# Time-step projection of a hybrid encoder with the tokens stationary and 32 weight columns moving

## The chip, the core and the metric

The kernel runs on one core of a Trainium2 chip. The metric is the device time of one execution in microseconds (us). TensorE (PE) multiplies a stationary tile, which it loads first, with columns that move through it, and sums into banks of PSUM; VectorE (DVE), ScalarE (ACT) and GpSimd (POOL) work on tiles in SBUF and PSUM; SyncE (SP) issues most of the transfers (DMA).

## What is computed

An encoder of two layers over 512 tokens of width 1024, in float32. Each layer has a feed-forward block, three token mixers in parallel (a Mamba-2 state-space branch, an S5 branch, a retention branch) with gates, and a second feed-forward block. The change touches the first step of the state-space branch, which makes one step size `dt` for each token, direction and head:

```python
h = rmsnorm(x, mix_norm[i])
proj = h @ w_in[i]
z, xbc, dt_raw, u, q, k, v, g, gate_logits = jnp.split(proj, split_pts, axis=-1)
...
dt = jax.nn.softplus(dt_raw.astype(f32).reshape(b, s, 2, SSD_HEADS) + dt_bias.astype(f32))
```

`dt_raw` has 2 x 8 = 16 columns out of 6800 of `proj`. From `dt` come the decays of the scan over chunks of 128 tokens.

## The kernel before

The activations lie with the model width on the partitions: `hh[k]` and `hl[k]`, k = 0 to 7, are the high and the low part of 128 rows of the normed input by 512 tokens, in fp32r. Products are made of such parts to keep the precision: `mm3` (L154 to L158) makes high x high, high x low and low x high. Nearly all large projections take a 128 x 128 piece of the weights as the stationary tile and move 512 tokens through it; their rows carry L156, L157 and L158. Weights are loaded by `wload` in pieces of 512 KB, three buffers deep, and split by ACT (`whi`, L149) and DVE (`wlo`, L150).

`ssd` (L507) is the state-space branch. Its weights for `dt`, `wdt`, hold for each k 32 columns, 16 of the high and 16 of the low part. Before the change the 32 columns are the stationary tile, all 512 tokens move, and the result stands with the columns on 32 partitions (`pdt`). ACT copies it to SBUF (`dts`, L525), PE transposes it in four pieces into a second small bank (`ptd`, L528), so that the tokens lie on the partitions, and DVE copies it out (`dt2`, L530). Then DVE adds the halves, scales by the norm (`rtd`) and adds the bias (L532, L534), and works out the softplus with some 40 small operations (L477 to L505), `da` (L540) and its parts. PE sums the decays (L549). Behind it follow six convolutions (`proj_dt`, `pad` L570, L575, transposes L587), the chunk states (L605), and per chunk the stages with `gm` (L626), `e` (L661), the sums of decays (L657) and the product with `e` (L664).

Between these, `hook()` puts one block of the S5 branch at a time (`s5_block`, L992): `mat` comes by DMA, PE forms L1009, DVE and POOL scan, DVE writes `h` (L1036, L1037), PE forms L1041 and L1043. `gates` (L1048) gives projections that fill the time between.

The order of the instructions on each engine is fixed when the program is built: a scheduler lists them by its own estimate of durations. So a change of one step can move others. PSUM has four banks for large products (`mm`), two small ones (`sm`) and one each of `pa` and `pb`.

The column sums of the norm (`norm_fin`, L194) are named in the prediction because of their shape: 128 x 128 of the squares stationary, two columns of ones moving.

Of the kernel before, what the change touches and what calls it, by code (L numbers as in the profile page):

```python
# [10 lines left out]
F32 = mybir.dt.float32  # L11
F32R = mybir.dt.float32r
I32 = mybir.dt.int32
AF = mybir.ActivationFunctionType
# [4 lines left out]
P = 128  # L19
D = 1024  # L20
KD = D // P
S = 512
# [79 lines left out]
class Core:  # L102
# [404 lines left out]
    def ssd(self, i, L, xs, hook=lambda: None):  # L507
        nc = self.nc
# [3 lines left out]
        with self.tc.tile_pool(name="ssd", bufs=1) as sp:  # L512
# [4 lines left out]
            nc.sync.dma_start(wst, w[:, DT0:DT0 + 16].rearrange("(k p) n -> p k n", p=P))  # L517
            wdt = sp.tile([P, KD, 32], F32R, name="dtw2")
            self.split(wdt[:, :, 0:16], wdt[:, :, 16:32], wst)
            pdt = self.bank("sm")  # L520
            for k in range(KD):
                nc.tensor.matmul(pdt[:32], wdt[:, k], self.hh[k], start=k == 0, stop=False)
                nc.tensor.matmul(pdt[:16], wdt[:, k, 0:16], self.hl[k], start=False, stop=k == KD - 1)
            dts = sp.tile([32, S], F32, tag="y", name="dts", bufs=3)
            nc.scalar.activation(dts, pdt[:32], AF.Copy)  # L525
            ptd = self.bank("sm")
            for t in range(NT):
                nc.tensor.transpose(ptd[:, 32 * t:32 * t + 32], dts[:, t * P:(t + 1) * P], self.id[:32, :32])  # L528
            dt2 = sp.tile([P, NT, 2, 16], F32, name="dt2")
            nc.vector.tensor_copy(dt2.rearrange("p t j d -> p (t j d)"), ptd[:, :P])  # L530
            raw = sp.tile([P, NT, 16], F32, name="dtraw")
# [65 lines left out]
            for d, order in ((0, (0, 1, 2, 3)), (1, (3, 2, 1, 0))):  # L597
                for ci in range(3):
                    t, tn = order[ci], order[ci + 1]
# [618 lines left out]
```

## Time and profile before

| | before |
|---|---|
| median of 3 runs | 2577.45 us (2576.88 to 2578.72) |
| profiled execution | 2580.19 us, of which its span 2578.4 us |
| PE busy | 2538.3 us (98%), 12044 matmul records |
| weight loads of PE (PEld) | 2104.0 us (82%) |
| DVE busy | 1514.7 us (59%) |
| ACT busy | 878.3 us (34%) |
| POOL busy | 646.9 us (25%) |
| DMA | 286.34 MB, mean 111 GB/s |

Shares are of the span. PEld runs beside PE. Matmuls follow each other before the one ahead has ended, so a record of 0.39 us can stand for a step of 0.23 us: the distance between starts is what counts. A matmul with plain fp32 operands leaves two records. PEclk is the clock of PE that was granted, as a share of full speed (2.4 GHz); 0.50 is 1.2 GHz.

### The profile page before, as it was taken

How to read it: one execution, taken by the hardware profiler on the slowest of the kernel's cores; microseconds unless marked ns; L12 is line 12 of the kernel's file. 1: busy time of each engine (PE TensorE's matmuls, PEld its weight loads, DVE VectorE, ACT ScalarE, POOL GpSimd, SP SyncE). 2: the span in 40 equal slices, each digit the busy share in tenths (PEclk: the TensorE clock that was granted, in tenths of full speed). 3: DMA queues.
4: the chain of work that ended last, by engine and by line, in shares of the span. 5: the costliest groups of instructions: out<-in, count | busy, mean ns of one | idle time of the engine just before them, and what ended most of it. 6: DMA issues, size and time to landing. Idle time of an engine off the chain costs nothing. (4 is left out here: it accounts for less than half of the span.)

```text
span 2578.4 us, 31738 instructions
## 1 busy us (share of the span) xinstructions
PE 2538.3 (98%) x12044; PEld 2104.0 (82%) x12044; DVE 1514.7 (59%) x2462; ACT 878.3 (34%) x1298; POOL 646.9 (25%) x636
## 2 busy tenths in 40 slices
PE   8999999999999999999999999999999999999998
PEld 6878887778888888888887888887878888888886
DVE  7746746897555644333486377478965556433433
ACT  4324433334333432222333243333343333322222
POOL 3203411462233221011112043105613323210110
PEclk9999999989999999999999999999899999999999
DMA  5434435342423433332334344454324234324322
GB/s 155 128 116 137 145 120 162 115 129 65 130 78 83 119 98 89 106 98 88 102 89 142 113 148 138 132 144 127 108 69 126 82 82 121 100 82 114 98 83 81
DMA packets 451832, 286.34 MB, mean 111 GB/s; under 512 B 29152, under 2 KB 435296, under 8 KB 451680
## 3 DMA queue, kind: packets, MB, share of 16 engines
q1 hardware_dynamic: 447456, 281.26, 36.7%
q10 hardware_dynamic: 4224, 3.06, 0.4%
q8 instruction: 95, 1.56, 0.2%
q14 instruction: 57, 0.47, 0.1%
HBM read 251.24 MB, written 29.88 MB: 109 GB/s over the span
## 5 line engine op out<-in xcount | busy, mean ns | idle before, releaser
L149 ACT ACTIVATE whi<-wst 128x1024 fp32r<-128x1024 f32 (+4 forms) x488 | 451.6, 927 | 1136.0 <-PE ps_mm L157 906.2
L156 PE MATMUL ps_mm<-hh,whi 128*128 128x512 f32 x1936 | 760.6, 393 | 6.4 <-ACT whi L149 3.7
L158 PE MATMUL ps_mm<-hh,wlo 128*128 128x512 f32 x1936 | 763.9, 395 | 2.6 <-DVE wlo L150 2.6
L157 PE MATMUL ps_mm<-hl,whi 128*128 128x512 f32 x1936 | 761.7, 394 | 0.0
L150 DVE TENSOR_TENSOR wlo<-wst,whi 128x1024 fp32r<-128x1024 f32 (+4 forms) x488 | 558.4, 1145 | 247.3 <-ACT whi L149 246.3
L156 PEld LDWEIGHTS ps_mm<-hh,whi 128*128 128x128 f32 x1936 | 366.2, 189 | 84.2 <-ACT whi L149 4.9
L158 PEld LDWEIGHTS ps_mm<-hh,wlo 128*128 128x128 f32 x1936 | 365.8, 189 | 79.4 <-DVE wlo L150 3.7
L157 PEld LDWEIGHTS ps_mm<-hl,whi 128*128 128x128 f32 x1936 | 365.9, 189 | 77.6 <-issue 1.7
L227 POOL TENSOR_TENSOR sr<-gt,rbc 128x512 f32<-128x512 f32 x88 | 149.1, 1696 | 817.9 <-ACT gt L225 817.9
L158 PE MATMUL ps_mm<-ah,wlo 128*128 128x512 f32 x704 | 275.6, 391 | 3.1 <-DVE wlo L150 3.1
L157 PE MATMUL ps_mm<-al,whi 128*128 128x512 f32 x704 | 274.6, 390 | 0.0
L156 PE MATMUL ps_mm<-ah,whi 128*128 128x512 f32 x704 | 274.1, 390 | 0.0
L229 DVE TENSOR_TENSOR a<-ps_mm,sr 128x512 f32<-128x512 f32 x88 | 60.4, 687 | 178.8 <-PE ps_mm L158 167.5
L158 PEld LDWEIGHTS ps_mm<-ah,wlo 128*128 128x128 f32 x704 | 132.4, 188 | 31.1 <-DVE wlo L150 3.9
L157 PEld LDWEIGHTS ps_mm<-al,whi 128*128 128x128 f32 x704 | 132.4, 188 | 28.2 <-DVE al L162 0.6
L156 PEld LDWEIGHTS ps_mm<-ah,whi 128*128 128x128 f32 x704 | 132.6, 188 | 27.9 <-ACT ah L161 0.7
L224 DVE TENSOR_TENSOR gt<-ps_mm,rbc 128x512 f32<-128x512 f32 x88 | 60.1, 686 | 139.7 <-PE ps_mm L158 139.6
L157 PE MATMUL ps_mm<-wlo,hh 128*128 128x512 f32 x320 | 126.3, 395 | 0.0
L156 PE MATMUL ps_mm<-whi,hh 128*128 128x512 f32 x320 | 125.9, 400 | 0.0
L158 PE MATMUL ps_mm<-whi,hl 128*128 128x512 f32 x320 | 125.5, 392 | 0.0
L245 DVE SCALAR_TENSOR_TENSOR x<-ps_mm,x 128x512 f32<-128x512 f32 x64 | 44.3, 692 | 133.7 <-PE ps_mm L158 133.4
L184 POOL TENSOR_TENSOR sqsum<-sqsum,sqk 128x512 f32<-128x512 f32 x42 | 67.4, 1606 | 191.0 <-ACT sqk L183 190.7
(395 smaller groups left out, 3257.2 us busy)
## 6 DMA issues: line engine op xcount, KB each, us to landing
wst<-in_ffn_w_gate SPq DMA_DIRECT2D x87, 512.0 KB, 3.7
wst<-in_ffn_w_up SPq DMA_DIRECT2D x87, 512.0 KB, 3.7
wst<-in_w_in SPq DMA_DIRECT2D x74, 512.0 KB, 3.7
wst<-in_ffn_w_down SPq DMA_DIRECT2D x64, 384.0 KB, 3.1
wst<-in_ffn_w_down SPq DMA_DIRECT2D x64, 320.0 KB, 3.1
wst<-in_w_in SPq DMA_DIRECT2D x64, 256.0 KB, 3.0
mat<-sd SPq DMA_DIRECT2D x12, 896.0 KB, 5.1
sd<-mat SPq DMA_DIRECT2D x12, 768.0 KB, 5.0
```

The source lines that it names most:

```text
L149: nc.scalar.activation(hi[:, :nk * n], sv, AF.Copy)
L150: nc.vector.tensor_tensor(lo[:, :nk * n], sv, hi[:, :nk * n].bitcast(F32), ALU.subtract)
L156: mm(out, lh, rh, start=first, stop=False)
L157: mm(out, lh, rl, start=False, stop=False)
L158: mm(out, ll, rh, start=False, stop=last)
L184: nc.gpsimd.tensor_tensor(self.sq, self.sq, t, ALU.add)
L224: nc.vector.tensor_tensor(gt, pg, self.rbc, ALU.mult)
L227: nc.gpsimd.tensor_tensor(sr, gt, self.rbc, ALU.mult)
L229: nc.vector.tensor_tensor(a, pu, sr, ALU.mult)
L245: nc.vector.scalar_tensor_tensor(self.x[d], pd, 0.5, self.x[d], ALU.mult, ALU.add)
```

## The change

The 128 tokens of a chunk become the stationary tile, and the 32 columns of `wdt` move. For each of four chunks there are sixteen matmuls, eight with `hh` and 32 columns and eight with `hl` and 16 columns, which sum into 32 columns of one small bank. The result has the tokens on the partitions at once; the bank `pdt`, the copy `dts` and the four transposes are gone. From the copy out of PSUM on all is as before, two lines higher up in the file (L530 becomes L528, L570 becomes L568, and so on).

```diff
-            pdt = self.bank("sm")
-            for k in range(KD):
-                nc.tensor.matmul(pdt[:32], wdt[:, k], self.hh[k], start=k == 0, stop=False)
-                nc.tensor.matmul(pdt[:16], wdt[:, k, 0:16], self.hl[k], start=False, stop=k == KD - 1)
-            dts = sp.tile([32, S], F32, tag="y", name="dts", bufs=3)
-            nc.scalar.activation(dts, pdt[:32], AF.Copy)
             ptd = self.bank("sm")
             for t in range(NT):
-                nc.tensor.transpose(ptd[:, 32 * t:32 * t + 32], dts[:, t * P:(t + 1) * P], self.id[:32, :32])
+                tc_ = slice(t * P, (t + 1) * P)
+                for k in range(KD):
+                    nc.tensor.matmul(ptd[:, 32 * t:32 * t + 32], self.hh[k][:, tc_], wdt[:, k], start=k == 0, stop=False)
+                    nc.tensor.matmul(ptd[:, 32 * t:32 * t + 16], self.hl[k][:, tc_], wdt[:, k, 0:16],
+                                     start=False, stop=k == KD - 1)
```

On PE, in the first layer, before (`dtw` is the tile of `wdt`; the last transposes of the step follow 22 large matmuls later):

```order
L157 MATMUL ps_mm<-hl_3481,whi 128x512
L158 MATMUL ps_mm<-hh_3480,wlo 128x512
L522 MATMUL ps_sm<-hh_3075,dtw_3648 32x512
L523 MATMUL ps_sm<-hl_3076,dtw_3648 16x512
L522 MATMUL ps_sm<-hh_3132,dtw_3648 32x512
L523 MATMUL ps_sm<-hl_3133,dtw_3648 16x512
```

At the same place after:

```order
L157 MATMUL ps_mm<-hl_3481,whi 128x512
L158 MATMUL ps_mm<-hh_3480,wlo 128x512
L524 MATMUL ps_sm<-dtw_3648,hh_3075 128x32
L525 MATMUL ps_sm<-dtw_3648,hl_3076 128x16
L524 MATMUL ps_sm<-dtw_3648,hh_3132 128x32
```

The place is the same; 16 matmuls before and 64 after stand there one behind the other, with nothing between, in both layers.

On DVE, where the result is taken out of PSUM, before (`pad` and `cacc` belong to the first convolution, `spt` to the softplus):

```order
L530 COPY dt_3675<-ps_sm 128x128
L532 TENSOR_TENSOR dtraw<-dt_3675 128x64
L570 TENSOR_TENSOR pad<-ps_mm,rbc 128x512
L534 SCALAR_TENSOR_TENSOR dtraw<-dtraw,rtd,dtb 128x16 x4
L150 TENSOR_TENSOR wlo<-wst,whi 128x1024
L492 TENSOR_SCALAR spt<-dtraw 128x64
L575 SCALAR_TENSOR_TENSOR cacc<-pad,vec_86,cacc 128x512
L493 TENSOR_TENSOR spt<-spt,dtraw 128x64
```

And after, the copy and the piece in which the first `pad` comes:

```order
L528 COPY dt_3716<-ps_sm 128x128
L530 TENSOR_TENSOR dtraw<-dt_3716 128x64
L532 SCALAR_TENSOR_TENSOR dtraw<-dtraw,rtd,dtb 128x16 x4
L492 TENSOR_SCALAR spt<-dtraw 128x64
L493 TENSOR_TENSOR spt<-spt,dtraw 128x64
```

```order
L497 TENSOR_TENSOR spt<-spt 128x64
L498 TENSOR_TENSOR spt<-spt 128x64
L568 TENSOR_TENSOR pad<-ps_mm,rbc 128x512
L500 TENSOR_SCALAR dt<-spt 128x64
L502 SCALAR_TENSOR_TENSOR dt<-dt,spt 128x64
```

The first `pad` has moved from the third place behind the copy to behind 26 operations of the step, and the convolution's operations no longer alternate with the first part of the softplus.

On PE, in the first layer, at the first products with `e`, before (`sst` are chunk states, `rb` the decays):

```order
L657 MATMUL ps_sm<-rb,us_r 128x512 x2
L1043 MATMUL ps_pb<-h,mat_4282 128x64 x2
L1041 MATMUL ps_pb<-uc,mat_4282 128x64
L1043 MATMUL ps_pb<-h,mat_4282 128x64 x2
L1041 MATMUL ps_pb<-uc,mat_4282 128x64
L1043 MATMUL ps_pb<-h,mat_4282 128x64 x2
L1041 MATMUL ps_pb<-uc,mat_4282 128x64
L1043 MATMUL ps_pb<-h,mat_4282 128x64 x2
L1009 MATMUL ps_pa<-uc,mat 128x64 x8
L664 MATMUL ps_sm<-xs,e 128x64 x4
L657 MATMUL ps_sm<-rb,ls_r 128x512 x2
```

After, ahead of the same products:

```order
L157 MATMUL ps_mm<-hl_3365,whi 128x512
L158 MATMUL ps_mm<-hh_3364,wlo 128x512
L156 MATMUL ps_mm<-hh_3422,whi 128x512
L662 MATMUL ps_sm<-xs,e 128x64 x4
L655 MATMUL ps_sm<-rb,ls_r 128x512 x2
L655 MATMUL ps_sm<-rb,us_r 128x512 x2
```

Between the first decays (L655 x4, L657 before) and the products with `e` there now stand 37 large matmuls and one L1039 (L1041 before); the S5 matmuls that stood there have moved to other places.

## Rows read from the trace of the kernel before

**Rows 1.** The page's first table: engine, busy us (share), records.
```profile
PE 2538.3 (98%) x12044; PEld 2104.0 (82%) x12044; DVE 1514.7 (59%) x2462; ACT 878.3 (34%) x1298; POOL 646.9 (25%) x636
```

**Rows 2.** PE's waits from 400 to 650, then 1700 to 1910: total, times, longest.
```profile
PE ps_pb L1043 <- DVE h L1037: 2.2, 3, 1.3
PE ps_sm L664 <- DVE e L661: 1.5, 2, 1.0
PE ps_sm L631 <- DVE gm L626: 1.3, 1, 1.3
...
PE ps_pb L1043 <- DVE h L1037: 2.5, 3, 1.3
PE ps_sm L664 <- DVE e L661: 1.5, 4, 0.7
PE ps_sm L631 <- DVE gm L626: 0.8, 1, 0.8
```

**Rows 3.** Timeline of PE: start, us, line, out<-in, stationary tile, moving tile, count.
```profile
422.15 0.40 PE L522 MATMUL ps_sm<-hh,dtw 128*32 128x512 f32 x1
...
425.85 0.39 PE L156 MATMUL ps_mm<-hh,whi 128*128 128x512 f32 x1
```

**Rows 4.** Timeline of PE at the four transposes.
```profile
430.61 0.39 PE L156 MATMUL ps_mm<-hh,whi 128*128 128x512 f32 x1
430.93 0.43 PE L528 MATMUL ps_sm<-con,dts 32*128 32x32 f32 x4
...
431.86 0.40 PE L156 MATMUL ps_mm<-hh,whi 128*128 128x512 f32 x1
```

**Rows 5.** Timeline of PE at the column sums of the norm (L194).
```profile
413.46 0.25 PE L194 MATMUL ps_sm<-ones_r,sqh 128*128 128x2 f32 x1
...
414.13 0.48 PE L158 MATMUL ps_mm<-hh,wlo 128*128 128x512 f32 x1
```

**Rows 6.** Timeline of PE at fp32r pairs with 64 stationary columns.
```profile
213.07 0.22 PE L156 MATMUL ps_sm<-xh,ch 128*64 128x128 f32 x1
...
213.79 0.44 PE L156 MATMUL ps_mm<-hh,whi 128*128 128x512 f32 x1
```

**Rows 7.** Timeline of PE at small fp32 matmuls, at full and at half clock.
```profile
459.10 1.22 PE L1009 MATMUL ps_pa<-uc,mat 128*128 128x64 f32 x10
460.15 0.39 PE L549 MATMUL ps_sm<-da,ls_r 128*128 128x64 f32 x2
...
1777.48 1.92 PE L1009 MATMUL ps_pa<-uc,mat 128*128 128x64 f32 x8
```

**Rows 8.** Stretches: length, busy us (records) by engine, PEclk, DMA share, GB/s.
```profile
520.00:540.00 20.00, 18.37 (x92) 15.98 (x91) 18.68 (x28) 8.27 (x9) 13.73 (x15) 0.83 0.47 145
560.00:600.00 40.00, 36.00 (x165) 30.68 (x163) 38.37 (x57) 11.43 (x16) 26.45 (x29) 0.83 0.27 79
1770.00:1860.00 90.00, 85.58 (x415) 72.67 (x414) 79.42 (x130) 28.72 (x35) 50.40 (x51) 0.85 0.43 134
```

**Rows 9.** The same view of short stretches.
```profile
526.00:529.00 3.00, 1.82 (x15) 1.68 (x14) 3.00 (x3) 2.97 (x3) 3.00 (x2) 0.94 0.42 111
1776.00:1782.00 6.00, 6.00 (x27) 5.82 (x28) 1.02 (x4) 1.67 (x2) 1.04 (x2) 0.50 0.54 176
423.00:426.00 3.00, 3.00 (x15) 1.45 (x13) 2.00 (x3) 0.18 (x1) 0.00 (x0) 1.00 0.26 97
459.00:462.00 3.00, 3.00 (x30) 2.96 (x28) 2.96 (x4) 2.52 (x3) 0.13 (x2) 1.00 0.05 11
```

**Rows 10.** Timeline of DVE around the copy out of PSUM.
```profile
429.36 1.12 DVE L886 TENSOR_TENSOR uu<-ps_mm,rbc 128x512 f32<-128x512 f32 x1 [2.25 <-DMA ud<-uu]
431.39 0.29 DVE L530 COPY dt<-ps_sm 128x128 f32<-128x128 f32 x1 [0.92 <-PE ps_sm L528]
...
451.29 1.52 DVE L502 SCALAR_TENSOR_TENSOR dt<-dt,spt 128x64 f32<-128x64 f32 x6
```

## Prediction

> **What bounds the kernel now.** I read the engine table of the page first: TensorE (PE) is busy for 2538.3 of 2578.4 us, on 98% of the span, and nothing else comes near [rows 1]. So time added to PE's queue is added to the kernel, unless it falls into one of the few places where PE waits. Next I read the list of PE's waits around the two state-space stages, one in each layer: the three largest on VectorE (DVE) are 2.2 + 1.5 + 1.3 = 5.0 us in the first layer and 2.5 + 1.5 + 0.8 = 4.8 us in the second [rows 2]. They lie behind the changed step, in stretches in which DVE is all but saturated: 18.7 of 20 us, 38.4 of 40 and 79.4 of 90 [rows 8]. In these the granted clock averages 0.83, 0.83 and 0.85, that is 0.17 x 20 + 0.17 x 40 + 0.15 x 90 = 3.4 + 6.8 + 13.5 = 24 us of full-speed PE time not given. The changed step itself runs in a stretch without any PE wait and at clock 1.00 [rows 3, 9]. So the change is judged by what it does to PE's queue there, then by what that does to the clock, and last by what reaches the waits of the state-space stage.
>
> **PE time removed.** Per layer the 16 matmuls of L522 and L523 start at 422.15 and the next large matmul at 425.85: 3.70 us, 0.23 us each [rows 3]. The four transposes stand between large matmuls: from the start at 430.61 to the one at 431.86 three large matmuls take 1.25 us instead of 3 x 0.23 = 0.68, so the transposes cost 0.57 us [rows 4]. Together 4.27 us of PE time per layer go.
>
> **PE time added.** 64 matmuls come, each with a stationary tile of 128 columns of its own and 32 or 16 moving columns. The trace has no such shape, but two neighbours. The column sums of the norm (L194) have the same stationary tile and 2 moving columns: they follow each other at 0.112 us, six steps from 413.46 to 414.13 [rows 5]. The start matrices of the S5 branch and the decay sums (L1009, L549), 64 moving columns and two records for each instruction, run at the same pace: ten records from 459.10 to 460.15, 0.105 us each [rows 7]. Between 2 and 64 moving columns the step doesn't change, so the load of the 128 stationary columns sets it, and 32 columns lie between. The bound from below is a pair with half the stationary columns (64) and 128 moving: twelve of them in 213.07 to 213.79, 0.06 us each [rows 6]. I take 0.114, with a little for the edges: 64 x 0.114 = 7.3 us per layer. Net 7.3 - 4.27 = +3.0 us per layer, **+6.1 us** for both; at 0.06 it would be 3.84 - 4.27 = -0.4 per layer, -0.9 in all.
>
> The Trainium skill speaks for the change here. The page "TensorE: Matmul & The Clock Gate", section "Back-to-back issue gap", gives some 60 cycles, about 25 ns, for a matmul of 1 to 64 moving columns; by that, as an estimate, 64 x 0.025 = 1.6 us, 2.7 us less than now per layer, and the kernel would end near 2572. The 0.112 us of a matmul with 2 moving columns in this trace is against it, since there each matmul brings its own load.
>
> **The clock.** The new run puts 7.3 us of load-paced matmuls with few columns in one piece. In this trace the clock began to fall in 526 to 529 (0.94), where PE was busy for 1.82 of 3.00 us, with 64-column matmuls. More telling is 1776 to 1782: PE is busy without any gap, 6.00 of 6.00 us, nearly all load-paced small matmuls, and the clock stays at 0.50 [rows 9]. So busy time in this form doesn't bring the clock back. Against a fall: 459 to 462, also load-paced and without a gap, kept 1.00 [rows 9]; but that is some 3 us between large matmuls, with twice and four times the moving columns. The new run is twice as long and has fewer columns than any of these, so I expect that the clock falls to 1.2 GHz in it, and comes back after some large matmuls. At 0.50 both sorts slow down: eight L1009 records take 1.92 us [rows 7], twice what they take at 1.00. A fall thus costs half of the low stretch. In windows of 2 us I count five low stretches in the two stages, so the 24 us make 4.8 us each [rows 8]. One in each layer: **+9.6 us**, between 0 (no fall) and 2 x 6.8 = 13.6, by the one that lies in 560 to 600.
>
> **What hides nothing, and what might give back.** The ACT copy (0.59 us) and the second small PSUM bank go; ACT isn't waited for there, I cost that at nothing. On DVE no instruction is added or removed, and the copy out of PSUM (L530), now at 431.39, is freed: the last of the 64 matmuls ends near 429.5 at full clock, near 431 to 433 at half. The third of the `uu` products stands ahead of it on DVE until 430.5 [rows 10], so at best it begins 0.9 us earlier. The order of the changed program puts 26 operations of the softplus chain ahead of the first convolution, where they were interleaved with it one by one. The large matmuls behind the run are later by the 3 us and by the clock's loss, so DVE finds time for this chain before the first `pad`; alone each costs 0.25 us (six in 1.52) [rows 10], some 6 us, about the time that PE needs for the first projection. DVE is then ahead of PE by a few us when the saturated stage begins, and PE's waits on it shrink. Of the 5.0 and 4.8 us I take some 40%, **-4 us**; the bounds are 0 and -9.8.
>
> **The sum.** +6.1 + 9.6 - 4 = +11.7 us. The profiled execution took 2580.2 us, 1.8 outside its span, and is 2.7 above the median of 2577.45 of the three runs; a difference of stages applies to both alike. Forecast 2577.45 + 11.7 = **2589 us**, +0.45%. Its own range: with the cheapest fall (3.4 us in each layer) and all waits gone 6.1 + 6.8 - 9.8 = +3.1, 2580.5; with the dearest and nothing given back 6.1 + 13.6 = +19.7, 2597.
>
> **Rivals.**
> *The clock holds.* PE has no gap in the new run, and 459 to 462 kept 1.00 [rows 9]. Then +6.1 - 4 = +2.1: 2579.6, at most 2583.6. It decides by whether 1.00 stands throughout the run. The same page of the Trainium skill, section "Why this matters for your kernels", asks for no more than that PE isn't left idle between bursts; by that rule this rival is right. The stretch from 1776 to 1782 doesn't agree with it.
>
> *The re-planned stage gives back more than the step costs (faster).* The planner has re-ordered the whole state-space stage; the first four products with `e` (L664), which stood directly behind eight L1009 and ahead of four L657, now have 37 large matmuls between them and the L657 before. If DVE's lead and this fill end all these waits (9.8) and half of the lost clock (12 of 24), 21.8 us come back: 6.1 + 9.6 - 21.8 = -6.1, 2571. It decides where the waits and falls of the stages are cut by more than 15.7 + 5.2 = 21 of their 34 us. Against it: the dense groups of small matmuls are still there, in other places, and DVE has the same work.
>
> *The re-planned stage waits more.* DVE stays saturated, several loads of `mat` have changed places with loads of weights in SyncE's queue, and an order that fits the planner's durations need not fit the chip's: as many waits again as now, +9.8, makes 2577.45 + 15.7 + 9.8 = 2603; with half, 2598.
>
> *The loads hide.* At 0.06 us a matmul and without a fall: -0.9, 2576.6. Only the pairs with half the stationary tile speak for it; L194 speaks against it.
>
> **Chances.** Forecast 0.58, clock holds 0.20, faster by the stage 0.12, more waits 0.08, loads hide 0.02. A measurement of this kernel can tell about 0.2%, 5.2 us, from no change. Slower by more than that: most of the forecast (0.52), more waits (0.08), a quarter of the held clock (0.05): 0.65. Within: 0.06 + 0.15 + 0.02 = 0.23. Faster: 0.12. The range leaves out the faster case and the far end of the waits: 2576 to 2599.
>
> **What would show it.** Right: 64 PE matmuls at 0.11 us in one piece, later at twice that; granted clock below 1.00 within some us of 429 and 1701; the large matmuls behind it at 0.43 us; PE's busy time higher by about 15 us; DVE's copy near 431. Wrong: steps of 0.06 us or less; 1.00 throughout; or PE's waits on `h`, `e`, `gm` and `sst` and the stage's mean clock changed by more than the step itself costs, in which case the order and not the shape has set the result.

## The result

The changed kernel takes 2606.52 us (median of 4 runs, 2602.29 to 2608.74) against 2578.09 of the kernel before beside it (4 runs, 2576.88 to 2579.68): ratio 1.0108, 95% interval 1.009 to 1.0125, slower by 28.4 us. The forecast was 2589 with a range up to 2599. Its direction was right and its size wrong: 28.4 us came where 11.7 were forecast. The traced execution took 2608.74 us with a span of 2606.9.

The engine table of the page after answers rows 1:

```profile
PE 2563.6 (98%) x12132; PEld 2131.7 (82%) x12132; DVE 1517.1 (58%) x2462; ACT 874.4 (34%) x1294; POOL 652.4 (25%) x636
```

PE is busy for 25.3 us more, on 98% of the span as before, and idle for 3.2 us more. In the changed kernel L528 is DVE's copy, L1041 the matmuls with `h`, L662 those with `e`. The timeline of PE in the first layer's run of 64 matmuls, which answers rows 3:

```profile
425.35 0.26 PE L525 MATMUL ps_sm<-dtw,hl 128*128 128x16 f32 x1
425.46 0.35 PE L524 MATMUL ps_sm<-dtw,hh 128*128 128x32 f32 x1
425.64 0.36 PE L525 MATMUL ps_sm<-dtw,hl 128*128 128x16 f32 x1
...
432.05 0.36 PE L525 MATMUL ps_sm<-dtw,hl 128*128 128x16 f32 x1
432.26 0.77 PE L156 MATMUL ps_mm<-hh,whi 128*128 128x512 f32 x1
432.83 0.63 PE L157 MATMUL ps_mm<-hl,whi 128*128 128x512 f32 x1
433.26 0.63 PE L158 MATMUL ps_mm<-hh,wlo 128*128 128x512 f32 x1
```

The steps are 0.11 us until 425.5, then 0.21; the large matmuls behind take 0.43 us from start to start. The windows over the same place (the columns of rows 8; the clock is the third number from the end) show the fall, with PE and its weight loads busy without a gap. They answer rows 9:

```profile
420.00:424.00 4.00, 4.00 (x27) 3.30 (x26) 2.27 (x3) 1.06 (x1) 0.00 (x0) 1.00 0.31 93
424.00:428.00 4.00, 4.00 (x28) 4.00 (x27) 1.75 (x2) 0.00 (x0) 0.00 (x0) 0.69 0.72 223
428.00:432.00 4.00, 4.00 (x20) 4.00 (x21) 1.11 (x1) 0.00 (x0) 0.00 (x0) 0.50 0.30 109
432.00:436.00 4.00, 4.00 (x11) 3.24 (x12) 3.18 (x17) 0.00 (x0) 0.00 (x0) 0.53 0.47 101
436.00:440.00 4.00, 4.00 (x19) 3.27 (x18) 2.81 (x11) 0.56 (x1) 0.00 (x0) 1.00 0.80 96
```

DVE's copy begins at 432.45, somewhat behind the forecast's 431. So far this is the forecast. What the forecast did not have is the state-space stage behind. PE's waits around it, first layer and then second, which answer rows 2:

```profile
PE ps_pb L1041 <- DVE h L1035: 7.4, 5, 2.8
PE ps_sm L662 <- DVE e L659: 2.6, 1, 2.6
...
PE ps_pb L1041 <- DVE h L1035: 7.2, 5, 2.2
PE ps_sm L662 <- DVE e L659: 2.2, 4, 0.8
```

PE's waits on `h` and `e` grew from 3.7 and 4.0 us to 10.0 and 9.4, where the forecast had them shrink. But they are now the only ones in these stretches: in the kernel before PE also waited for `gm`, `sst`, `mat` and others, 8.0 and 6.6 us with `h` and `e`. All waits together grew by 4.8 us only. The stage itself, from its first matmul with `uc` to its last with `h`, as windows of the kernel before:

```profile
459.10:602.40 143.30, 136.61 (x720) 114.98 (x718) 131.95 (x212) 50.17 (x60) 86.37 (x92) 0.93 0.36 111
1730.70:1876.70 146.00, 140.55 (x720) 117.30 (x718) 131.10 (x210) 50.29 (x60) 86.33 (x92) 0.91 0.35 109
```

and of the changed kernel:

```profile
469.20:624.80 155.60, 145.63 (x711) 122.21 (x710) 130.78 (x208) 48.00 (x60) 90.71 (x91) 0.87 0.35 104
1755.60:1914.40 158.80, 149.13 (x743) 123.74 (x742) 136.31 (x213) 50.51 (x64) 88.72 (x92) 0.90 0.34 104
```

It became 12.3 and 12.8 us longer, with nearly the same DVE work in the first layer (130.78 us against 131.95) and a lower granted clock. Of the 25.1 us PE is idle for 7.5 and busy for 17.6, so most of it is not waiting. Not all of it is loss, since the new order puts other large matmuls between the two ends; the first transposes of the retention behind it start 18.0 us later in the first layer (784.4 against 766.4) and 28.5 us later in the second (2069.5 against 2041.0).

### The profile page after: what moved, and what is told of

Its sections match the earlier page's. It is cut to its first block, busy times and chain, and to the rows that moved or that the text cites. A ratio compares the mean times of both kernels' runs of the same rounds, so it can differ in the third digit from the quotient of the medians.

```text
span 2606.9 us, 31903 instructions
## 1 busy us (share of the span) xinstructions
PE 2563.6 (98%) x12132; PEld 2131.7 (82%) x12132; DVE 1517.1 (58%) x2462; ACT 874.4 (34%) x1294; POOL 652.4 (25%) x636
## 4 chain that ended last, share of the span: by engine, by line
PE 88%; DVE 6%; POOL 2%; DMA 1%; issue 1%; ACT 1%; SPq 1%; ACTq 0%; DVEq 0%; POOLq 0%
PE ps_mm L158 26%; PE ps_mm L156 26%; PE ps_mm L157 26%; DVE wlo L150 1%; PE ps_pa L1007 1%; PE ps_pb L1041 1%; DVE bm L645 1%; PE ps_sm L421 1%; PE ps_pa L429 1%; PE ps_sm L386 1%; PE ps_pa L428 0%; DVE rb L651 0%; PE ps_sm L954 0%; PE ps_sm L662 0%; PE ps_sm L629 0%
```

## The experiments

Two edits are mixed in the changed kernel: the step, and the new order that the planner gave everything behind it. The experiments take them apart. Each experiment kernel says for every engine in which order its instructions stand, and ties each instruction to the one ahead of it on the same engine. Such a tie carries no semaphore; the old order with cover, which has the step of before, leaves 31738 instructions in its trace, as many as the kernel before. A kernel tied to its own unchanged order was not timed.

```diff
+ORDER = {"PE": "...", "DVE": "...", "Activation": "...", "Pool": "...", "SP": "..."}
+def pin(nc, tc):
+    for s in ORDER.values():
+        seq = ...   # numbers of the instructions in the program's text, in the wanted order
+        for a, b in zip(seq[:-1], seq[1:]):
+            tc.add_manual_dep(ins[b], ins[a].name, no_sync, reason="order")
...
     with tile.TileContext(nc, schedule_with_timeline_sim=True) as tc:
         hybrid_encoder_kernel(tc, aps, out)
+        pin(nc, tc)
```

The pinned kernels have three lines more at their top, so L1044 here is L1041 of after where the step is new, and L1046 where it is old.

| kernel | median us | ratio to before, 95% interval | PE waits of 0.3 us and more, both stages, us | at half clock in both stages, us |
| --- | --- | --- | --- | --- |
| before | 2577.5 | 1 | 13.7 | 47.8 |
| after | 2606.5 | 1.0108 (1.009 to 1.0125) | 19.2 | 75.2 |
| new step, old order | 2591.2 | 1.0053 (1.004 to 1.0065) | 12.6 | 47.8 |
| old step, new order | 2599.8 | 1.008 (1.0068 to 1.0093) | 23.1 | 61.5 |
| new step spread, old order | 2583.7 | 1.0024 (1.0015 to 1.0033) | 15.4 | 37.6 |
| narrow tiles, old order | 2573.4 | 0.9985 (0.9976 to 0.9994) | 13.3 | 47.8 |
| step left out, old order | 2573.9 | 0.9983 (0.9973 to 0.9993) | 15.7 | 44.4 |
| POOL works for `h` first, new order | 2599.5 | 1.0088 (1.0074 to 1.0102) | 22.7 | 47.9 |
| new order with cover | 2596.7 | 1.007 (1.0058 to 1.0082) | 16.5 | 37.6 |
| old order with cover | 2575.1 | 0.999 (0.9982 to 0.9998) | 18.2 | 13.6 |
| old step early | 2575.5 | 0.9982 (0.9974 to 0.9991) | 14.3 | 37.6 |

The kernel before ran beside each group of kernels, with medians of 2576.6 to 2578.9 us; its first row is one of them, and the ratios go by the executions beside each. The last two columns are of the one traced execution of each kernel; the falls of the clock in the dt runs are not in them. The time at the half clock is added up from windows of 1 us (a window at 0.75 counts for half of it). Single executions of one kernel lie up to 12 us apart (the step left out: 2566.49 to 2578.10) and the lists of falls differ from trace to trace, so these two columns are read for their large differences alone. The narrow tiles and the step left out do less work than the others, as told below.

### New step, old order

The 64 matmuls stand where the 16 wide ones stood, and the copy and the transposes are gone; all else is kept in the order of before.

> The changed step (64 matmuls with their own 128-column stationary tile per layer) in the place where the 16 wide matmuls stood, no copy and no transposes; every other instruction of every engine is kept in the order of the kernel before. Theory 1 (the loss beyond the step comes from the order that the planner chose for the state-space stage): only the step's own price is left, 6.1 us for the added matmuls and 8.5 us for the two falls of the clock, 2577.5 + 14.6 = 2592 us (2588 to 2597), ratio 1.0057; the waits of PE on DVE's h and e stay near 5.6 us in layer 0 and 5.4 us in layer 1. Theory 2 (the later and slower step upsets the stage whatever the order): as the changed kernel, 2606 us (2600 to 2609), ratio 1.011, waits of some 10 us in each layer.

Measured: 2591.23 us, ratio 1.0053. The waits on DVE are those of before, with nearly the same lengths: the longest is 1.34 us for `h`, where before had 1.33. The two largest rows of PE's waits in the first layer, which answer rows 2:

```profile
PE ps_pb L1044 <- DVE h L1038: 2.6, 4, 1.3
PE ps_sm L665 <- DVE e L662: 1.5, 3, 0.9
```

The first run and its fall are as in the changed kernel (10.2 us at the half clock, 6.8 in the second layer). So the step costs 13.7 us (10 to 17 by the interval), and the remaining 15.3 us of the changed kernel went with its order. Theory 1 held, theory 2 fell. How the order costs them is in the engine table of this trace:

```profile
PE 2552.3 (99%) x12132; PEld 2119.3 (82%) x12132; DVE 1514.2 (58%) x2462; ACT 876.8 (34%) x1296; POOL 647.8 (25%) x636
```

PE is busy for 14.0 us more than before, which is the step's price. The changed kernel, with the same 12132 records, is busy for another 11.3 us and idle for another 4.7, which make the 16.0 us between the two spans (2606.9 against 2590.9). So in these traces the order costs mostly through PE's lower clock, and the smaller part by waiting.

### Old step, new order

The reverse: the step of before, the order of after.

> The step as it was before (16 wide matmuls, ACT's copy, 4 transposes 22 large matmuls later), and every other instruction of every engine in the order of the changed kernel. Theory 1 (the order costs the rest): 2577.5 + 14 = 2591 us (2587 to 2597), ratio 1.0054, waits of PE on DVE's h and e near 10 us in layer 0 and 9 us in layer 1, and more than 60 us at the half clock in the two state-space stages. Theory 2 (the step costs all): 2577.5 us (2575 to 2580), ratio 1.000.

Measured: 2599.79 us, ratio 1.008, a second trace 2596.58. The new order costs 22 us without the new step, more than the 14 forecast and outside the range of theory 1, which had it up to 2597. Theory 2, with no cost at all, falls. The large waits stand where they stand in the changed kernel; here the timeline of PE at them in the changed kernel (the number in brackets is the idle time before the instruction):

```profile
495.04 0.43 PE L1041 MATMUL ps_pb<-h,mat 128*128 128x64 f32 x2 [2.44 <-DVE h L1035]
541.84 0.69 PE L1041 MATMUL ps_pb<-h,mat 128*128 128x64 f32 x2 [2.77 <-DVE h L1035]
597.08 1.33 PE L662 MATMUL ps_sm<-xs,e 128*128 128x64 f32 x5 [2.60 <-DVE e L659]
```

and in this one:

```profile
488.94 0.43 PE L1046 MATMUL ps_pb<-h,mat 128*128 128x64 f32 x2 [2.44 <-DVE h L1040]
535.84 0.43 PE L1046 MATMUL ps_pb<-h,mat 128*128 128x64 f32 x2 [2.79 <-DVE h L1040]
585.57 1.76 PE L667 MATMUL ps_sm<-xs,e 128*128 128x64 f32 x7 [2.60 <-DVE e L664]
```

2.44, 2.77 and 2.60 us there, 2.44, 2.79 and 2.60 here: the same waits to 0.02 us, though the step ahead of them is another and they begin 6 to 12 us earlier. They belong to the order. Beside them this kernel waits for `wlo` (1.29 us, and 1.91 in the second layer) and for `da` (0.67 and 1.14), 5.0 us that the changed kernel doesn't have. The two prices, 13.7 and 22, don't add up to 28.4; these waits may be part of the reason, but that isn't shown: both traced executions have them and lie at 2595.0 and 2596.6, the quick end of this kernel.

> The same kernel as old_step_new_order, for a second trace, since its executions lay between 2595 and 2601 us and the traced one at the low end: the waits of PE should stand at the same places with the same lengths (2.44, 2.8 and 2.6 us in layer 0), and what differs should be the number or length of the falls of the clock, in steps of 3.4 us at the half clock, 1.7 us each.

The second trace has the same waits to 0.02 us in the first layer (2.44, 2.79, 2.60). Its falls have other lengths at the same places (13.7 and 3.4 us where the first had 10.2 and none), with the same sum of 61.5 us. So the three longest waits repeat, single falls don't. Not every wait repeats: in the second layer `h` is waited for 1.29 us in one trace and 2.01 in the other, and a wait of 2.15 us stands only in the second.

### The step spread among large matmuls

The 64 matmuls stand one by one between 512-column matmuls, from 411 to 435 us in the first layer, in a bank of their own.

```diff
-            ptd = self.bank("sm")
+            ptd = self.bank("pa")
```

> The changed step with its 64 matmuls per layer set one by one between 512-column matmuls of the projections around it, into a bank of its own, so that no run of short matmuls is left; all else in the order of the kernel before. Theory 1a (each short matmul costs its 0.111 us wherever it stands, the clock's fall costs the rest): no record at the half clock between 408 and 436 us, 2577.5 + 6.1 = 2583.6 us (2581 to 2587). Theory 1b (in the run it was the stationary tile's load that set the 0.111 us, and behind a 512-column matmul the load is hidden, so that only the 32 columns' share of 0.227 us, 0.014 us, is left): 2577.5 + 2 x (64 x 0.014 - 4.27) = 2570.7 us (2568 to 2575), faster than the kernel before, ratio 0.9974. If the clock falls all the same: 2588 us or more.

Measured: 2583.74 us, ratio 1.0024: 6.2 us above before (4 to 8.5 by the interval), as theory 1a has it. The clock stays at 1.00 from 410 to 436. The trace agrees: from the first column sum of the norm to the first matmul with `uc` it is 46.25 us before (412.85 to 459.10) and 49.33 here (411.14 to 460.47), 3.08 more in each layer. With the 64 matmuls in one piece (new step, old order) it takes 54.00 and 52.34, another 4.67 and 3.01: that is the price of the two falls. The timeline of PE shows the pairs:

```profile
414.33 0.18 PE L527 MATMUL ps_pa<-dtw,hh 128*128 128x32 f32 x1
414.35 0.47 PE L160 MATMUL ps_mm<-hl,whi 128*128 128x512 f32 x1
414.66 0.17 PE L528 MATMUL ps_pa<-dtw,hl 128*128 128x16 f32 x1
414.69 0.48 PE L161 MATMUL ps_mm<-hh,wlo 128*128 128x512 f32 x1
```

and that of its weight loads:

```profile
414.33 0.19 PEld L160 LDWEIGHTS ps_mm<-hl,whi 128*128 128x128 f32 x1
414.44 0.19 PEld L528 LDWEIGHTS ps_pa<-dtw,hl 128*128 128x128 f32 x1
```

The short matmul and its next large one stand 0.02 us apart, but the load of the large tile begins only with the short matmul (414.33), and the next load 0.11 us after that. A pair takes 0.34 us: 0.23 and 0.11. A short matmul with a wide tile of its own costs 0.11 us in either place; the fall of the clock came only with the run.

### Narrow tiles

> The changed step in the order of the kernel before, but with 56 of the 64 matmuls per layer holding only 32 columns of the stationary tile (the first 32 tokens of each 128; the time steps of the other tokens are left without 7 of 8 chunks and are not those of the reference); the moving 32 and 16 columns are the same. Theory L (the stationary tile's load sets the 0.111 us, and grows with its columns): a narrow matmul takes less than 0.08 us at the full clock, the run lasts some 5 us instead of 10, and the time lies 2 to 8 us under the 2591 us of the full run. Theory F (a fixed price for each short matmul whatever its columns): 0.111 us each, the same run of 10 us with its fall of the clock, 2591 us (2588 to 2594).

```diff
+                    n = P if k == 0 else 32
+                    tn = slice(t * P, t * P + n)
-                    nc.tensor.matmul(ptd[:, 32 * t:32 * t + 32], self.hh[k][:, tc_], wdt[:, k], ...)
+                    nc.tensor.matmul(ptd[:n, 32 * t:32 * t + 32], self.hh[k][:, tn], wdt[:, k], ...)
```

The kernel leaves out seven of eight chunks for 96 of every 128 tokens, so its time steps are not those of the reference.

Measured: 2573.39 us, ratio 0.9985, 17.8 us below the full run in the same order, where 2 to 8 were forecast for theory L. The timeline of PE, with tiles of 128 columns and then 32:

```profile
423.77 0.26 PE L530 MATMUL ps_sm<-dtw,hl 128*128 128x16 f32 x1
423.88 0.18 PE L529 MATMUL ps_sm<-dtw,hh 128*32 128x32 f32 x1
423.92 0.18 PE L530 MATMUL ps_sm<-dtw,hl 128*32 128x16 f32 x1
...
424.33 0.48 PE L159 MATMUL ps_mm<-hh,whi 128*128 128x512 f32 x1
```

0.11 us with 128 stationary columns, 0.03 with 32, at the same 32 and 16 moving columns: the step goes with the stationary columns. The run lasts 2.6 us, and the clock stays at 1.00. That accounts for the whole: (7.1 - 2.6) x 2 = 9.0 us of matmuls and (10.2 + 6.8) / 2 = 8.5 us of clock are 17.5. The Trainium skill, page "TensorE: Matmul & The Clock Gate", section "LDWEIGHTS (loading the stationary operand)", gives a load time that goes with the columns of the tile alone, columns over 1.2 in ns, which as an estimate is 107 and 27 ns; the trace agrees with 0.111 and 0.031 us.

### The step left out

```diff
-                for k in range(KD):
-                    nc.tensor.matmul(ptd[:, 32 * t:32 * t + 32], self.hh[k][:, tc_], wdt[:, k], ...)
-                    nc.tensor.matmul(ptd[:, 32 * t:32 * t + 16], self.hl[k][:, tc_], wdt[:, k, 0:16], ...)
+                nc.tensor.matmul(ptd[:, 32 * t:32 * t + 32], self.hh[7][:, tc_], wdt[:, 7], start=True, stop=True)
```

> The step is left out but for 4 matmuls per layer (one 128-row chunk of 8, upper half alone, so that the time steps are not those of the reference), no copy and no transposes; all else in the order of the kernel before. What the old step cost on the path: by the rows of before 3.70 us of wide matmuls and 0.57 us of transposes per layer, against 4 x 0.111 us that stay, 2577.5 - 2 x 3.83 = 2569.8 us (2568 to 2572), ratio 0.9970, if all of it lies on the path. If PE's later waits take it back: 2575 to 2578 us, ratio 0.999 to 1.000.

The kernel leaves out all of the step but one chunk of eight, so its time steps are not those of the reference either.

Measured: 2573.85 us, ratio 0.9983 (0.9973 to 0.9993), a gain of 3.7 us between medians, between the two forecasts. The traces show where the rest is. This is the first column sum of the norm before, where the first matmul with `uc` follows at 459.10 [rows 7]:

```profile
412.85 0.17 PE L194 MATMUL ps_sm<-ones_r,sqh 128*128 128x2 f32 x1
```

and these are both here:

```profile
409.73 0.17 PE L197 MATMUL ps_sm<-ones_r,sqh 128*128 128x2 f32 x1
452.16 1.22 PE L1007 MATMUL ps_pa<-uc,mat 128*128 128x64 f32 x10
```

46.25 us became 42.43, and as much in the second layer: 3.82 and 3.81 less, against the 3.83 of the rows. So all that the step took lay on the path. Behind that the trace loses 0.6 us again up to the column sums of the second layer, and 2.1 from the second layer's first matmul with `uc` to its retention. This retention begins 8.0 us earlier than before (2033.0 against 2041.0), but 3.1 of these were there ahead of the step (409.73 against 412.85), since executions differ in their opening. The narrow tiles are level with this kernel between medians, though by the same two marks they gain only 1.61 us per layer; what the stage takes back, and why, was not tried.

### Cover at the waits

If the waits are the price of the new order, other work ahead of the waiting matmuls must take it away. In the changed kernel's order the next 8 to 12 large matmuls are taken ahead of the six longest waits; in the old order 3 to 6 at eight places of each layer. At the first of the six places the order of PE changes in this way:

```diff
 L158 ps_mm<-whi,hl
+11 large matmuls (L156 to L158) that stood behind the L1007
 L1041 ps_pb<-h
 L1039 and L1041, 9 more
 L603 ps_sm<-xw,btd, 4
 L1007 ps_pa<-uc, 8
-11 large matmuls (L156 to L158)
```

> The changed kernel in its own order, but at the six places where PE waited longest for DVE's h or e in its trace (2.44, 2.77, 2.60, 2.00, 1.57 and 2.17 us, 13.6 us together) the next 8 to 12 large matmuls of the projections are taken ahead of the waiting one. Theory 1 with its mechanism (the new order's price is these waits and the falls of the clock that follow each): waits gone and the stages' time at the half clock back from 75 us to some 48 us, 2606.5 - 14 = 2592 us (2588 to 2597). If the clock falls because of the bursts of short matmuls alone, the waits go and the falls stay: 2606.5 - 10 = 2597 us (2594 to 2601). If the waits only move to the places that the large matmuls were taken from: 2606 us (2602 to 2610).

> The kernel before, step and order, but at the eight places of each layer's state-space stage where PE waited over 0.4 us in one layer or the other (11.2 us together) the next 3 to 6 large matmuls are taken ahead of the waiting one. If each wait is a cost and calls the fall of the clock behind it: 2577.5 - 11 = 2566 us, and down to 2543 us if the 47.8 us at the half clock of the two stages go too (23.9 us lost there). If the falls come from the bursts of short matmuls: 2566 us (2563 to 2570). If the waits only move: 2577 us (2573 to 2581).

Measured: 2596.68 us for the new order, 9.8 below the changed kernel; 2575.05 us, ratio 0.999, for the old one, between the forecasts of 2566 and 2577. The stages as windows, of the new order with cover:

```profile
467.50:613.60 146.10, 136.72 (x712) 112.22 (x711) 133.96 (x208) 47.95 (x60) 86.78 (x91) 0.95 0.37 111
1748.00:1901.10 153.10, 145.61 (x754) 119.97 (x752) 134.57 (x211) 49.76 (x62) 88.71 (x91) 0.94 0.35 107
```

and of the old order with cover:

```profile
458.60:600.20 141.60, 133.61 (x722) 109.52 (x721) 131.33 (x210) 49.85 (x60) 85.94 (x92) 0.98 0.36 112
1728.50:1870.10 141.60, 133.65 (x722) 109.56 (x721) 131.33 (x210) 49.85 (x60) 85.94 (x92) 0.98 0.36 112
```

In the new order the first stage is 9.5 us shorter than in the changed kernel (146.1 against 155.6) and the clock is 0.95 instead of 0.87; the sum of the waits fell only from 19.2 to 16.5 us. So the time lies within theory 1 and within its rival of the bursts, and the mechanism of neither is seen whole: the sum of the waits stayed near, and the time at the half clock fell by half. In the old order the clock rises from 0.93 and 0.91 to 0.98, the time at the half clock falls from 47.8 to 13.6 us, which at half its length would be worth 17 us. The stages became 1.7 and 4.4 us shorter and the waits 4.5 us longer, as the forecast has it for waits that only move; the largest is 2.77 us for `e` at 582.9.

So the falls do not follow the sum of the waits: here they nearly vanish while the waits grow. What starts a fall in this stage stays open. And a fall isn't worth half its length there: PE is busy for 11.1 us less than before (2527.2 against 2538.3) but idle for 4.6 more, and between medians only 2.4 us are left. DVE is busy for 131.3 of 141.6 us (93%), so what PE gains from the clock it may then wait for DVE; that is argued from these rows, no run isolates it.

### The step and DVE's chain earlier

The prediction's give-back rested on a head start of DVE. Here the old step gets one: its matmuls begin at 409 instead of 422 us, and DVE's 40 operations from the copy to `dal` fill gaps that DVE had before.

```diff
-            pdt = self.bank("sm")
+            pdt = self.bank("pa")
-            ptd = self.bank("sm")
+            ptd = self.bank("pb")
 DVE, by lines of the kernel before:
 L202 dg x4, L150 wlo
+L530, L532, L534 x4, L492, L493
 L206 rbc, L886 uu, L150 wlo
+L477 to L480
 L886 uu
+L485, L481, L482, L484 x6
 L886 uu
+L486, L495 to L498, L500, and the other 13 one by one behind the L575
```

> The kernel before with the step of the time steps earlier: its 16 wide matmuls set ahead of the sums of squares (some 12 us earlier, into a bank of its own), copy and transposes behind them, and DVE's 40 small operations of that chain filled into the gaps that DVE had before 431 us; all else in the order of before. Theory A (the DVE head start that the prediction counted with 4 us: what DVE does earlier it need not do in the state-space stage, so PE waits less there): 2573.5 us (2568 to 2576), ratio 0.9984, waits of PE on DVE's h and e in the two stages fall from 7.7 us to under 4 us. Theory B (PE's waits in the stage are set by where the static order puts PE's short matmuls against the last DVE operations ahead of them, which a few us of DVE time earlier do not move): 2577.5 us (2575 to 2580), ratio 1.000, the same waits at the same places. If the moved operations hold up a weight split that PE needs: over 2580 us.

Measured: 2575.45 us, ratio 0.9982 (0.9974 to 0.9991), which is in the ranges of both theories. The waits are those of theory B. They stand where they were: 1.05 us for `e` at 568, 1.34 for `h` at 571, 1.09 for `gm` at 573, against 1.01, 1.33 and 1.27 before; those on `h` and `e` are 6.3 us in the two layers, against 7.7, and not under 4. But little of the head start reaches the stage: DVE writes `da` at 450.0 us instead of 456.5, and `dal`, the last of the chain, at 456.4 instead of 457.0. Run again:

> early_dt once more, beside other executions of the kernel before, since its gain of some 3.5 us is near what a measurement can tell and the two later variants that contain its edit lay at 2575.3 and 2576.7 us: if the gain is real, ratio 0.998 to 0.999 and 2573 to 2576 us again; if it was the draw of the executions of before, ratio 0.9995 to 1.0005.

2574.85 us, ratio 0.9993 (0.9984 to 1.0002). A gain of 2 to 4 us at most, not settled by these runs, and not seen in the waits. Besides the old order with cover it is the only version of the same computation whose interval lay below 1, in the first of its two runs. Both edits together, and with less cover:

> Both edits to the order of the kernel before at once: the step of the time steps and DVE's chain earlier (early_dt) and the large matmuls taken ahead of the eight waits per layer (old_order_cover). If DVE sets the pace of the stage once the falls of the clock are gone: the head start now counts in full, 2575.0 - 4 = 2571 us (2568 to 2574). If the two edits gain from the same place: 2575 us (2573 to 2577), as either alone.

> early_dt with fewer large matmuls taken ahead, at five places per layer instead of eight (3, 3, 5, 5 and 4 matmuls), so that fewer are missing behind. If the waits that old_order_cover showed behind the moved matmuls (2.77, 1.67 and 0.96 us per layer) came from taking too many: these shrink to under 1.5 us each, and the time is 2 to 6 us below early_cover, 2567 us (2564 to 2572). If it is only the waits of before again: 2575 us, as early_dt.

2575.30 us (ratio 0.9994, 0.9985 to 1.0003) and 2576.67 us (1.0003, 0.9994 to 1.0012): the two edits together gain no more than either alone, and less cover brought nothing. No version that is clearly faster than the kernel before was found.

### POOL works for `h` first

Why is `h` late in the new order? The timeline of DVE just ahead of the wait of 2.44 us in the changed kernel:

```profile
482.17 1.47 DVE L573 SCALAR_TENSOR_TENSOR cacc<-pad,vec,cacc 128x512 f32<-128x512 f32 x1
483.56 2.06 DVE L150 TENSOR_TENSOR wlo<-wst,whi 128x1024 fp32r<-128x1024 f32 x1
```

that of POOL there:

```profile
478.98 2.72 POOL L599 TENSOR_TENSOR xw<-xs,wds 128x512 f32<-128x512 f32 x2
481.66 1.42 POOL L617 TENSOR_TENSOR w__4239<-xs,dsk 128x512 f32<-128x512 f32 x1
483.05 1.49 POOL L617 TENSOR_TENSOR w__4252<-xs,dsk 128x512 f32<-128x512 f32 x1
484.50 1.72 POOL L1028 TENSOR_TENSOR ia<-it,mat 128x256 f32<-128x256 f32 x1
```

and DVE's weight split at the same place of the kernel with the new step in the old order, where POOL is idle from 480.6 to 485.4:

```profile
481.89 1.23 DVE L153 TENSOR_TENSOR wlo<-wst,whi 128x1024 fp32r<-128x1024 f32 x1
```

The new order has POOL do `xw` and `w` (5.5 us) ahead of the `ia` and `ib` that `h` is made of. POOL was idle at DVE's split in the old order, and busy at it in the new. The edit, for the first group of each layer:

```diff
 L1032 MEMSET h
+L1028 ia, L1029 ib, L1028 ia, L1029 ib
 L599 xw x2
 L617 w x2
-L1028 ia, L1029 ib, L1028 ia, L1029 ib
```

> The changed kernel in its own order, but on GpSimd (POOL) the four products ia and ib that DVE's h needs stand directly behind the zeroing of h in every group, ahead of the products xw, w, rb and bm that the new order puts first (four of them, 5.5 us, in the first group of each layer; one to three in five others); PE, DVE, ACT and the DMAs keep the changed kernel's order. Theory P (h is late in the new order since POOL does other work first, and DVE's own operations stretch beside it): PE's waits on h of 0.53 + 2.44 us at 490 to 495 and 0.61 + 2.00 us at 1777 to 1782 go, and those near 542 and 1829 (2.77 and 1.57 us) shrink; 2606.5 - 8 = 2598 us (2593 to 2602). Theory D (h is late since DVE comes to it late, whatever POOL does): the same waits, 2606 us (2602 to 2610).

Measured: 2599.46 us, ratio 1.0088, 7 us below the changed kernel, within the range of theory P. The waits on `h` of 0.53 + 2.44 and 0.61 + 2.00 us are gone. In their place PE now waits for `xw`, and the next wait on `h` didn't shrink but grew from 2.77 to 3.38:

```profile
485.45 0.65 PE L606 MATMUL ps_sm<-xw,btd 128*64 128x256 f32 x4 [2.89 <-POOL xw L602]
538.75 0.69 PE L1044 MATMUL ps_pb<-h,mat 128*128 128x64 f32 x2 [3.38 <-DVE h L1038]
```

But `h` itself came hardly earlier. These are POOL's last `ib` and DVE's last `h` of the first group, in the changed kernel and then in this one:

```profile
488.03 0.73 POOL L1029 TENSOR_TENSOR ib<-it,mat 128x256 f32<-128x256 f32 x1
494.57 0.42 DVE L1035 TENSOR_TENSOR h<-ia,ib 64x252 f32<-64x252 f32 x1
...
482.25 1.71 POOL L1032 TENSOR_TENSOR ib<-it,mat 128x256 f32<-128x256 f32 x1
493.21 1.17 DVE L1038 TENSOR_TENSOR h<-ia,ib 64x252 f32<-64x252 f32 x1
```

From the first matmul with `uc` (469.2 and 468.6 us), `ib` is done after 15.4 us instead of 19.6, and the last `h` after 25.8 us in both kernels (26.3 instead of 26.1 in the second layer). The wait on it went since PE, held up by `xw`, comes to it later. DVE's own order puts a copy that needs PE's product with `xw`, and a weight split of 2.06 us, ahead of this `h`. So POOL's order for `ia` and `ib` alone is not what makes `h` late; what DVE's order and its longer operations do to it was not tried apart. The sum of the waits rose from 19.2 to 22.7 us while the time at the half clock fell from 75.2 to 47.9. PE is busy for 12.5 us less than in the changed kernel (2551.1) and idle for 3.7 more: the gain came by the clock, which theory P did not have.

## Why the prediction was right in part and wrong in size

**The bound: right.** PE's queue set the time before and after, and PE's busy time rose by 25.3 us of the 28.4. Of the step alone it is 14.0, where the forecast had about 15.

**Time removed and added: right.** The matmuls took 0.111 us, against the 0.114 taken, and for the reason given, the load of the 128 stationary columns. The forecast was +6.1 us in all; the spread kernel, where the clock stays up, measures +6.2 (4 to 8.5 by its interval), and 3.08 per layer in its trace. The time removed is on the path to the stage in full, by the kernel without the step (3.82 of 3.83 us), and its median shows half of it.

**The clock: right.** The forecast was one fall in each layer, 4.8 us each; 10.2 and 6.8 us at the half clock are 5.1 and 3.4, 8.5 instead of 9.6; against the spread kernel they cost 4.67 and 3.01. In two other traces with the same run (new order with cover, POOL first) the second fall was 10.2 us long, so a part of the agreement in size is chance. The fall came in a stretch in which PE and its loads had no gap, as 1776 to 1782 had suggested [rows 9], so the rival that the clock holds fell with its reason.

**What gives back: wrong, and this is the step that failed.** The forecast was -4 us from a DVE that comes to the stage ahead of PE. In its place the new order cost some 15 us: 2606.5 against 2591.2 with nothing but the order between them, and 22 with the old step. The sum was then 6.1 + 9.6 = 15.7 against a measured 13.7 for the step, and -4 against +15 for the rest. The lead itself came, on the softplus chain: in the changed kernel DVE writes `dal`, the last of the chain, at 450.4 us, 18.8 ahead of the first matmul with `uc`, where before it was 457.0 and 2.1 ahead. What didn't hold is the link from the lead to the waits. PE's waits on `h` and `e` more than doubled, and the early chain left them at their places too. The prediction read the lead off one feature of the new order, 26 softplus operations ahead of the first convolution, and gave the rest of that order no price: the first product with `h`, which the lead should help, comes 21.1 us after the first matmul with `uc` (469.2 to 490.3), and 17.4 before (459.1 to 476.5). The second thing without a price is the stage's clock: the new order cost 11.3 us of PE's busy time at a lower clock and 4.7 us of idle time. The prediction's own last sign of being wrong names this, waits and a mean clock of the stage that change by more than the step costs. Which of the changed places in the order started the added falls stays open.

**The rival "the re-planned stage waits more" came nearest,** with a chance of 0.08 and a time of 2603. Its ground held: an order that fits the planner's durations need not fit the chip's. Its mechanism held in part: the waits on `h` and `e` grew by 11.7 us, but others went, so that all waits grew by about 5 us, and not by 9.8. The larger part came by the clock, which it did not count, so that its time was partly luck. The reason it was given so little is that the order was weighed by what looked better in it, and not taken as an unknown that can go either way by as much as the waits it touches; the faster rival, on the same unknown, got 0.12.

**The rule that a fall costs half its length** held nearly in the run of the 64 matmuls, where PE waits for nobody (4.67 and 3.01 us against 5.1 and 3.4). It doesn't hold in the state-space stage, by the old order with cover: 34 us less at the half clock, at most 5 us gained.

## What to carry to other kernels

A layout that turns few long matmuls into many short ones is priced by the stationary columns that each must load, wherever the short ones stand: 64 x 0.11 us here against 16 x 0.23, and in a row they also take the clock down. When a change is re-planned by a scheduler, the order behind it is a second change of its own: keep the old order on every engine and run the step alone, since here the order cost as much as the step (15 us and 14). And in a stage in which another engine is 93% busy, test what a wait or a fall of PE's clock is worth: here 34 us less at the half clock gave less than 5.

## What the runs showed of the hardware that was not expected

A short matmul between two long ones is not free: 0.34 us for a pair instead of 0.23. In the rows of the spread kernel the load of a large tile begins with the short matmul directly ahead and takes 0.11 us, of which only 0.02 lie behind that matmul.

DVE's operations take up to twice as long beside a busy POOL: the split of 128x1024 took 2.06 us while POOL was busy and 1.23 while it was idle, and the convolution's multiply-add 1.47 us, with 0.75 for the same operation when POOL rests. The long split began at 483.56, inside POOL's product of 483.05 to 484.54. Not each is longer: of 33 splits of the changed kernel during which POOL was busy nearly throughout, the middle one took 1.28 us. The Trainium skill, page "SBUF — State Buffer", section "SBUF: two separate sides", says that a DVE operation with two inputs in SBUF and a GpSimd operation that reads SBUF take one shared pair of ports in turn, each for a whole instruction; the rows of the long split agree with it. So an order can lengthen single DVE operations without adding any; in all, DVE's busy time grew by only 2.4 us (1517.1 against 1514.7).

Of one kernel, PE's three longest waits in the first layer were the same in two executions to 0.02 us, while the falls of its clock behind them came with other lengths (10.2 us at the half clock in one, 13.7 in the other).
